# RWKV outputs in tiles of their own, their projection rows during the attention, query-key chunks per pair, later transposes

## The chip, the cores and the metric

The kernel runs on one core of a Trainium2 chip. Its engines work side by side, each through its own queue of instructions in order: PE (TensorE, matrix products and transposes; its weight loads are counted apart as PEld), DVE (VectorE), ACT (ScalarE), POOL (GpSimd) and SP (SyncE, which issues the DMAs). The metric is the device time of one execution in microseconds (us), lower is better.

## The reference, cut to what matters

A decoder trunk of two layers over 512 positions of width 1024, with 256 memory tokens. Each layer normalizes, projects, runs three groups of heads, gates each group, concatenates and projects back. The change lies in the first, the even layer:

```python
def even_layer(h, km, vm, ...):
    qa, ka, va, ga, bs, gb, qm, gm = split_last(h @ w_in, EVEN_SIZES)
    qa = partial_rope(rms_norm(split_heads(qa, A_HEADS), a_qn_g), cos, sin)
    ka = partial_rope(rms_norm(split_heads(ka, A_HEADS), a_kn_g), cos, sin)
    oa = merge_heads(moba_attention(qa, ka, split_heads(va, A_HEADS)))
    ob = rwkv7_time_mix(bs, ...)
    om = memory_attention(rms_norm(split_heads(qm, M_HEADS), m_qn_g), km, vm)
    mixed = jnp.concatenate([oa * silu(ga), ob * silu(gb), om * silu(gm)], axis=-1)
    return mixed @ w_out          # x = x + this
...
    # end of rwkv7_time_mix: y (512 positions, 6 heads of 64)
    mean, var = jnp.mean(y, -1), jnp.mean(jnp.square(y - mean), -1)
    y = (y - mean) * rsqrt(var + eps) * lnx_g + lnx_b
    return y + bonus
```

There are 6 heads of attention, 6 of RWKV and 4 of memory attention, each 64 wide. At 512 positions the block-sparse attention is plain causal attention: a query's own block and all earlier ones are taken.

## The kernel before, in words

**Products.** Every projection is computed in three terms from operands split into a high and a low half (`hi`, `lo` of the weights, `act_hi`, `act_lo` of the activations). `weights` (line 244) brings a block of 256 columns by DMA in pieces of four 128-row tiles (`raw`), makes `hi` by a copy on ACT and `lo` by a subtraction on DVE; the pools are double buffered. `mm3` (line 263) issues the three terms; its matmul is line 269. `projT` makes outputs of 128 rows and 512 columns (24 multiplications), `projN` (line 280) outputs of 128 rows and up to 256 columns. Each output is a `pj` buffer in PSUM, of which there are two.

**The order.** A tile framework gives each engine its queue. Code in a `band` (line 291) has a priority: "g" ahead of "e" (what empties a result), the code's own order, "w" (weight halves), "n" (query and key norms) and "d" (projections). So the projections of a chunk are put between other work wherever the program order leaves PE a place, and nothing overtakes a waiting instruction once the queue is made.

**Even layer.** `first_part` and the rest are written in `even_layer` (line 1021). First come the chunks of the input projection in the order of the string `RWO` (line 40), each under the RWKV work: `l0 k0 r1 v1 r2 v2` are RWKV's inputs, `qm` the memory queries, `q1 q2 q3` and an early `q0` the four column blocks of 256 of queries, keys and values of the causal attention, `g0 g1` gates and values. `nat_chunk` (line 643) keeps a result with positions as rows in `nat0`, and `nat_norm` (line 469) normalizes two or four heads at a time and applies the rotation. A block `q1` holds two query heads and two key heads, `q0` four query heads, `q2` four key heads, `q3` values.

Then RWKV: for each pair of heads q = 0, 1, 2 `rwkv_out` (line 989) computes the outputs from the carried states, `Y` (line 998), subtracts the mean, squares on ACT, forms the reciprocal root in a chain of small DVE operations, scales (line 1010), transposes on PE (line 1013), adds the bonus and multiplies by the gate into `sg[3 + q]`. `Y` and `Yq` are one buffer each for the three q.

Then the attention, in units that `pipeline` (line 630) calls one after another, with steps due some units later (AD = 1 for causal units, ADM = 3 for memory units). `attn_mem_pair` (line 566) has two units for each of two pairs of memory heads: scores (line 503), minimum (line 581), exponential on ACT (line 584), scaling, transposes (line 600), the product with the values (line 609). `attn_causal_pair` (line 531) has four units for each of three pairs: scores, mask and minimum on DVE (line 513), exponential on ACT (line 515), scaling (line 542), transposes (line 549) with their copy to `PT` (527, 529), at the end the product with the values (line 557) and `mix` (line 520), which applies the gate. Before a pair is scored, `load(q)` calls `nat_T` (line 483) for its queries and its keys: four transposes each (line 486), a copy on ACT and a split on DVE (487, 488). `qT` and `kT` have two buffers, by q % 2. Before, `load(0)` was called ahead of all units, `load(1)` and `load(2)` at units and delays that the tuple `PO0` (line 38) gives.

**Output projection.** The gated results are act rows k = 0 to 7: 0 to 2 the three causal pairs, 3 to 5 RWKV, 6 and 7 memory. `split_act` (line 309) makes their halves. `first_part` (line 1144) splits rows 3 to 7 and calls `out_proj` (line 617) for them: four weight blocks of 256 columns, for each four groups of 15 multiplications and an add into `x` (line 623). It is called in the unit that `PO0` gives, 7, with delay 5. After the attention the same is done for rows 0 to 2, groups of 9. Then layer 1 begins with its norm and its transposes (line 461).

Of the kernel before, what the change touches and what calls it, by code (L numbers as in the profile page):

```python
# [11 lines left out]
F32R = mybir.dt.float32r  # L12
# [18 lines left out]
PD_ = 1000000  # L31
AD = 1
# [3 lines left out]
PO0 = (1, 1, 5, 2, 5)  # L36
PO1 = (1, 2, 5, 2, 8, 1, 11, 4, 4)
RWO = 'l0 k0 r1 v1 r2 v2 qm q1 g0 q2 q3 g1'
# [109 lines left out]
def tile_trunk(ctx, tc, x_in, memT_in, w_mem, e_w_in, e_w_out, o_w_in, o_w_out, ln_g, w2_in, a2_in,  # L148
# [95 lines left out]
    def weights(segs, k0=0, nk=KC):  # L244
# [3 lines left out]
        for ka in range(k0, k0 + nk, 4):  # L248
            kb = min(ka + 4, k0 + nk)
# [50 lines left out]
    def chunk(segs, body, k0=0, nk=KC, hot=False):  # L300
        if hot:
            hi, lo = weights(segs, k0, nk)
        else:
            with band("w"):
                hi, lo = weights(segs, k0, nk)
        with band("d"):
            body(hi, lo)
# [188 lines left out]
    def parts(pool, name):  # L496
        return [[tl(pool, [P, S], f"{name}{q}{c}", F32R) for c in "hl"] for q in range(2)]
# [119 lines left out]
    def out_proj(w, x, k0, nk, last=False):  # L617
        for c in range(4):
            def body(hi, lo, c=c):
                for i in range(NT):  # L620
# [6 lines left out]
                    projN(hi, lo, 0, 256, i, act_hi, act_lo, done, range(k0, k0 + nk))  # L627
            chunk([(w, 256 * c, 256)], body, k0, nk)
# [14 lines left out]
    def nat_chunk(w, wc, n, nat, c0, heads=(), hot=False):  # L643
# [16 lines left out]
        chunk([(w, wc, n)], body, hot=hot)  # L660
# [23 lines left out]
    qh = [[(0, 4, "aq")], [(0, 2, "aq"), (2, 2, "ak")], [(0, 4, "ak")], []]  # L684

    def qkv(c, hot=False):
        nat_chunk(ew, EV["qkv"] + 256 * c, 256, nat0, 256 * c, qh[c], hot)
# [12 lines left out]
    with ExitStack() as ph:  # L700
# [30 lines left out]
        qkv(0, True)  # L731
# [44 lines left out]
    def rwkv_tiles(rp):  # L776
        return dict(nr=tl(rp, [P, 4, S], "nr3"), pl=tl(rp, [P, 3, 8], "pl3"), bon=tl(rp, [P, 3, S], "bon3"),
# [211 lines left out]
    def rwkv_out(ip, X, q, sgb):  # L989
# [7 lines left out]
        Y = tl(ip, [P, 8, 64], "Y")  # L997
# [5 lines left out]
        sq = tl(ip, [P, 8, 64], "Yq")  # L1003
# [10 lines left out]
        yy = tl(ip, [P, S], "Yq")  # L1014
# [6 lines left out]
    def even_layer():  # L1021
        sg = [None] * 3 + sg0 + [None] * 2
        with ExitStack() as ph:
            rp = pool(ph, "rp")
            psum_pool(ph, "psr", 1)
            load_cst(rp, "mr", "bo2")
# [3 lines left out]
            X = rwkv_tiles(rp)  # L1030
# [51 lines left out]
            def gb2va(hi, lo):  # L1082
# [7 lines left out]
                q1=lambda: qkv(1), q2=lambda: qkv(2), q3=lambda: qkv(3),  # L1090
                g0=lambda: gate_chunk(ew, [(EV["gb"], sg[3]), (EV["gb"] + P, sg[4])]),
                g1=lambda: chunk([(ew, EV["gb"] + 256, P), (ew, EV["qkv"] + 1024, P)], gb2va),
                qm=lambda: nat_chunk(ew, EV["qm"], 256, qn0, 0, [(0, 4, None)]))
# [8 lines left out]
            with ExitStack() as ips:  # L1102
# [14 lines left out]
        with ExitStack() as ph:  # L1117
# [3 lines left out]
            qT = parts(np_, "qT")  # L1121
            kT = parts(np_, "kT")
            qmT = parts(np_, "qmT")
            for j in range(3):
                sg[j] = tl(np_, [P, S], f"sg{j}")
            gate_chunk(ew, [(EV["ga"], sg[0]), (EV["ga"] + P, sg[1])])
# [30 lines left out]
    with ExitStack() as ph:  # L1157
# [9 lines left out]
        out_proj(e_w_out, x1, 0, 3)  # L1167
# [320 lines left out]
```

## Time and profile before

| | |
|---|---|
| median of 3 runs | 660.4 us (660.39 to 661.84) |
| profiled execution | 660.36 us |
| its span | 658.6 us |
| granted PE clock, every slice | 0.9 or more of full speed |
| start, to 81 us | PE busy 81.00, DVE 60.11 |
| RWKV, 81 to 200 us | PE busy 117.96, DVE 92.75 |
| RWKV end, 228 to 262.14 us | PE busy 33.84 of 34.14, DVE 26.68 |

The span is the time from the first to the last instruction of the profiled execution; what lies around it is 1.8 us here. The windows quoted below give, for a stretch of the span, the busy time of each engine in it and its instructions in brackets. A row of a timeline gives the start, the duration, the engine, the line, the operation, output and inputs, shapes and how many such instructions were joined; a bracket behind it is idle time of the engine ahead of the row and what ended it. Durations of neighbouring matmuls overlap, so prices of them are taken from start to start.

### The profile page before, as it was taken

The numbers are of one execution on the slowest core, as the hardware profiler recorded it, in microseconds if no ns is written. First come the engines' busy times: TensorE is split into PE (matmuls) and PEld (weight loads), VectorE is DVE, ScalarE is ACT, GpSimd is POOL, SyncE is SP. The second block draws the span as 40 slices with busy tenths as digits, with TensorE's granted clock in tenths as the row PEclk, the third lists the DMA queues.
The fourth block names the chain that finished last, engine by engine and source line by source line (L and its number), as shares of the span: only waits on it lengthen the run. The fifth ranks groups of instructions, "written<-read, shape, count | busy, mean of one in ns | idle before, by whom it ended". The sixth has DMA issues, their size and how long they took to land.

```text
span 658.6 us, 15391 instructions
## 1 busy us (share of the span) xinstructions
PE 636.3 (97%) x6192; PEld 549.7 (83%) x6192; DVE 484.9 (74%) x1384; ACT 328.3 (50%) x969; POOL 6.0 (1%) x21
## 2 busy tenths in 40 slices
PE   8899999999999999889999999999999999999997
PEld 5788777898898878656999988779899689978997
DVE  3996775979786488998657985995786775688743
ACT  5567355552231135856425684644573665367220
POOL 1000000000000000000000000000000000000000
PEclk9999999999999999999999999999999999999999
DMA  8462223212220215100434424022232114200323
GB/s 293 135 184 56 66 65 95 72 50 81 66 67 3 66 33 166 42 18 25 136 97 128 124 77 127 3 69 89 71 97 65 34 34 127 65 33 1 97 65 127
DMA packets 62905, 53.52 MB, mean 81 GB/s; under 512 B 3377, under 2 KB 61041, under 8 KB 62834
## 3 DMA queue, kind: packets, MB, share of 16 engines
q1 hardware_dynamic: 62834, 52.55, 26.5%
q8 instruction: 48, 0.79, 0.5%
q14 instruction: 23, 0.19, 0.1%
HBM read 50.44 MB, written 2.10 MB: 80 GB/s over the span
## 4 chain that ended last, share of the span: by engine, by line
PE 70%; DVE 14%; ACT 11%; issue 2%; DMA 2%; SPq 0%; ACTq 0%; DVEq 0%
PE pj L269 52%; DVE lo L260 2%; ACT hi L259 2%; DMA raw<-in_o_w_in_dram 1%; PE s L503 1%; ACT pr L584 1%; PE s L920 1%; PE c L914 1%; PE t L609 1%; PE t L486 1%; ACT pr L515 1%; PE t L1353 1%; DMA memT<-in_memT_dram 1%; PE t L557 1%; PE s L943 1%
## 5 line engine op out<-in xcount | busy, mean ns | idle before, releaser
L259 ACT ACTIVATE hi<-raw 128x512 fp32r<-128x512 f32 (+2 forms) x164 | 89.3, 596 | 87.1 <-PE pj L269 79.1
L260 DVE TENSOR_TENSOR lo<-raw,hi 128x512 fp32r<-128x512 f32 (+2 forms) x164 | 101.2, 648 | 27.8 <-ACT hi L259 13.8
L269 PE MATMUL pj<-hi,act_hi 128*128 128x256 f32 x672 | 101.8, 285 | 0.8 <-ACT sq L654 0.7
L269 PE MATMUL pj<-hi,act_lo 128*128 128x256 f32 x672 | 101.7, 285 | 0.0
L269 PE MATMUL pj<-lo,act_hi 128*128 128x256 f32 x672 | 101.1, 284 | 0.0
L269 PEld LDWEIGHTS pj<-hi,act_hi 128*128 128x128 f32 x672 | 88.7, 188 | 2.8 <-ACT sq L654 0.9
L269 PEld LDWEIGHTS pj<-lo,act_hi 128*128 128x128 f32 x672 | 88.5, 189 | 1.7 <-issue 1.3
L269 PEld LDWEIGHTS pj<-hi,act_lo 128*128 128x128 f32 x672 | 88.6, 189 | 1.1 <-issue 0.6
L269 PE MATMUL pj<-act_hi,lo 128*128 128x512 f32 (+1 forms) x248 | 64.8, 403 | 0.0
L269 PE MATMUL pj<-act_hi,hi 128*128 128x512 f32 (+1 forms) x248 | 64.1, 400 | 0.2 <-ACT act_hi L461 0.2
L269 PE MATMUL pj<-act_lo,hi 128*128 128x512 f32 (+1 forms) x248 | 64.0, 400 | 0.0
L269 PEld LDWEIGHTS pj<-act_lo,hi 128*128 128x128 f32 (+1 forms) x248 | 45.4, 187 | 11.0
L269 PEld LDWEIGHTS pj<-act_hi,hi 128*128 128x128 f32 (+1 forms) x248 | 45.1, 187 | 10.7 <-ACT act_hi L461 0.5
L269 PEld LDWEIGHTS pj<-act_hi,lo 128*128 128x128 f32 (+1 forms) x248 | 44.8, 187 | 10.6 <-issue 0.4
L623 DVE TENSOR_TENSOR x<-pj,x 128x256 f32<-128x256 f32 x64 | 27.0, 422 | 34.1 <-PE pj L269 34.1
L654 ACT ACTIVATE sq<-pj 128x64 f32<-128x64 f32 x144 | 30.2, 229 | 25.4 <-DVE nat L529 15.7
L515 ACT ACTIVATE pr<-pr,mx 128x128 f32<-128x128 f32 (+3 forms) x56 | 31.2, 562 | 12.5 <-DVE mx L513 11.7
L654 ACT ACTIVATION_READ_ACCUMULATOR sq<-pj 128x1 f32 x144 | 29.4, 214 | 0.0
L513 DVE CUSTOM_DVE_ANT_0 pr<-s,mask 128x128 f32<-128x128 f32 (+3 forms) x56 | 25.8, 484 | 3.4 <-PE t L600 1.7
L466 ACT ACTIVATE th<-pj 128x512 f32<-128x512 f32 x16 | 9.6, 598 | 24.1 <-PE pj L269 24.0
L527 ACT ACTIVATE nat<-pj 128x256 f32<-128x256 f32 (+1 forms) x17 | 6.7, 397 | 27.8 <-PE pj L269 27.8
L527 ACT ACTIVATE PT<-t 128x512 f32<-128x512 f32 (+3 forms) x28 | 14.0, 499 | 10.1 <-PE t L600 5.8
(409 smaller groups left out, 1035.5 us busy)
## 6 DMA issues: line engine op xcount, KB each, us to landing
raw<-in_o_w_in_dram SPq DMA_DIRECT2D x20, 512.0 KB, 3.6
raw<-in_e_w_in_dram SPq DMA_DIRECT2D x36, 256.0 KB, 3.1
raw<-in_e_w_in_dram SPq DMA_DIRECT2D x10, 512.0 KB, 4.0
x<-in_x_dram SPq DMA_DIRECT2D x8, 512.0 KB, 7.1
raw<-in_o_w_in_dram SPq DMA_DIRECT2D x16, 256.0 KB, 3.7
raw<-in_o_w_out_dram SPq DMA_DIRECT2D x8, 512.0 KB, 3.4
raw<-in_e_w_out_dram SPq DMA_DIRECT2D x4, 512.0 KB, 3.5
raw<-in_w_mem_dram SPq DMA_DIRECT2D x4, 512.0 KB, 3.6
```

The costliest lines, as they stand in the source:

```text
L259: A.activation(hi[:, z, :n], r, AF.Copy)
L260: V.tensor_tensor(lo[:, z, :n], r, hi[:, z, :n].bitcast(F32), op=OP.subtract)
L269: T.matmul(o, lh(k), rh(k), start=c == 0, stop=c == tot - 1)
L466: A.activation(th, o, AF.Tanh, scale=0.5)
L486: T.transpose(t[:, i * P:(i + 1) * P], nat[:, i, c0:c0 + P], ident)
L503: T.matmul(o, qT[a][h, qs], kT[b][h, ks], start=c == 0, stop=c == 2)
L513: V.tensor_tensor_reduce(pr[:, p, :n], s[:, p, :n], mask[0][:, 384 - i * P:512], 1.0, 1e38, op0=OP.add, op1=OP.min, accum_out=mx[:, p:p + 1])
L515: A.activation(pr[:, p, :n], pr[:, p, :n], AF.Exp, bias=mx[:, p:p + 1], scale=-1.0, accum_out=rs[:, p:p + 1])
L527: A.activation(dst, src, AF.Copy)
L557: T.matmul(o[64 * p:64 * p + 64, j * P:], v[:, j, v0 + q * P + 64 * p:v0 + q * P + 64 * p + 64], PT[p][:, 4 * j:3 * j + 4, :].rearrange("p ...
L623: V.tensor_tensor(x[i][:, cs], o, x[i][:, cs], op=OP.add)
L654: A.activation(sq[:, h0 + h], o[:, 64 * (h0 + h):64 * (h0 + h + 1)], AF.Square, accum_out=ss[:, i * nh + h:i * nh + h + 1])
```

## The change

1. `rwkv_out` writes its results into slices of one tile `Y3` (under the name `AT3`, shared with an earlier buffer), one for each q, and takes its squares and its last product in buffers of different names for different q. The RWKV tiles are allocated ahead of the constants.
2. `first_part` takes act rows 3 to 5 alone, the RWKV outputs, and is called in the second memory unit with delay 0. The rows 6, 7, 0, 1, 2 (`EVK`) are projected in that order after the attention, in groups of 15. `weights`, `chunk` and `out_proj` take a list of rows.
3. The four column blocks `q0` to `q3` are cut otherwise: `pair(q)` holds the two query heads and the two key heads of pair q, from two places of the weights, and `v0` the values. `RWO` changes to `l0 k0 r1 v1 r2 v2 qm g0 g1 v0 q1 q2`, so the gates come ahead of the second and third pair.
4. `load(q)` is called later: `PO0` is gone, and ahead of each causal pair stand empty units, four before pair 0 and two before pairs 1 and 2, with `load(q)` due behind the last of them. So a pair's transposes come after the previous pair's product with the values.

```diff
+EVK = (6, 7, 0, 1, 2)
-PO0 = (1, 1, 5, 2, 5)
-RWO = 'l0 k0 r1 v1 r2 v2 qm q1 g0 q2 q3 g1'
+RWO = 'l0 k0 r1 v1 r2 v2 qm g0 g1 v0 q1 q2'
...
-    def out_proj(w, x, k0, nk, last=False):
+    def out_proj(w, x, ks, last=False):
...
-                first()
+                if first:
+                    first()
...
+    def pair(q, hot=False):
+        segs = [(ew, EV["qkv"] + 384 * j + P * q, P) for j in range(2)]
+        nat_chunk(segs, 256, nat0, 256 * q, [(0, 2, "aq"), (2, 2, "ak")], hot)
...
-    def rwkv_out(ip, X, q, sgb):
+    def rwkv_out(ip, X, q, Y3, sgb):
...
-        Y = tl(ip, [P, 8, 64], "Y")
+        Y = Y3[:, q]
...
-        sq = tl(ip, [P, 8, 64], "Yq")
+        t3 = lambda n: tl(ip, [P, 12, 64], n)[:, :8]
+        sq = t3(("xx", "F", "R1")[q])
...
-        yy = tl(ip, [P, S], "Yq")
+        yy = t3("R2" if q == 1 else "Yq").rearrange("p a t -> p (a t)")
...
-                    nat_T(nat0, q * P, gq["aq"], qT[q % 2])
-                    nat_T(nat0, 384 + q * P, gq["ak"], kT[q % 2])
+                    nat_T(nat0, 2 * q * P, gq["aq"], qT[q % 2])
+                    nat_T(nat0, (2 * q + 1) * P, gq["ak"], kT[q % 2])
...
-            load(0)()
+            def first_part():
+                for k in range(3, 6):
+                    split_act(k, sg[k])
+                out_proj(e_w_out, x1, range(3, 6))
...
-            us[PO0[0]][1].append((PO0[1], load(1)))
+            us[1][1].append((0, first_part))
             for q in range(3):
+                gap = ADM + 1 if q == 0 else AD + 1
+                us[-1][1].append((gap, load(q)))
+                us += [[None, []] for _ in range(gap)]
                 us += attn_causal_pair(ap, qT, kT, nat0, 768, q, sg[q])
...
-            us[PO0[2]][1].append((PO0[3], load(2)))
-            us[7][1].append((PO0[4], first_part))
             pipeline(us)
-            for k in range(3):
+            for k in EVK:
                 split_act(k, sg[k])
...
-        out_proj(e_w_out, x1, 0, 3)
+        out_proj(e_w_out, x1, EVK)
```

The change moves instructions on PE and on DVE. A row below has the line, the operation, output and inputs, the shape and how many such instructions stand in a row; line numbers of the kernel after are 3 to 8 higher. The first place is PE's queue in the last causal pair: transposes of probabilities (`pr`) and projections (`pj`). Before:

```order
L549 MATMUL t_4171<-cident,pr 128x128 x2
L269 MATMUL pj<-lo,act_hi 128x256 x5
L549 MATMUL t_4175<-cident,pr 128x128 x2
L269 MATMUL pj<-hi,act_hi 128x256 x5
L549 MATMUL t_4197<-cident,pr 128x128 x3
L549 MATMUL t_4202<-cident,pr 128x128 x3
L269 MATMUL pj<-hi,act_lo 128x256 x5
L269 MATMUL pj<-lo,act_hi 128x256 x5
L269 MATMUL pj<-hi,act_hi 128x256 x5
L269 MATMUL pj<-hi,act_lo 128x256 x5
L549 MATMUL t_4207<-cident,pr 128x128 x4
L549 MATMUL t_4213<-cident,pr 128x128 x4
```

And now, with the product with the values (64 rows) behind them:

```order
L552 MATMUL t_4120<-cident,pr 128x128
L552 MATMUL t_4141<-cident,pr 128x128 x2
L552 MATMUL t_4145<-cident,pr 128x128 x2
L552 MATMUL t_4167<-cident,pr 128x128 x3
L552 MATMUL t_4172<-cident,pr 128x128 x3
L552 MATMUL t_4177<-cident,pr 128x128 x4
L552 MATMUL t_4183<-cident,pr 128x128 x4
L560 MATMUL t_4189<-PT,nat 64x512 x2
L560 MATMUL t_4189<-PT,nat 64x384 x2
L560 MATMUL t_4189<-PT,nat 64x256 x2
L560 MATMUL t_4189<-PT,nat 64x128 x2
L272 MATMUL pj<-hi,act_hi 128x256 x2
```

Before, projections in groups of five rows stood between the transposes; now no projection stands between the transposes of the last pair, and the first ones of the last part (`hi`, `act_hi`) follow its product with the values.

The second place is PE's queue in the second pair of memory heads (`qmT1`, line 600 before and 603 now its transposes, `pj<-act…` the gates). Before:

```order
L486 MATMUL t_3429<-cident,nat 128x128 x4
L486 MATMUL t_3436<-cident,nat 128x128 x4
L269 MATMUL pj<-act_hi,hi 128x512 x8
L503 MATMUL s<-qn,qmT1h 128x256 x2
L503 MATMUL s<-qn,qmT1l 128x256 x2
L503 MATMUL s<-qn,qmT1h 128x256 x4
L503 MATMUL s<-qn,qmT1l 128x256 x2
L503 MATMUL s<-qn,qmT1h 128x256 x2
L600 MATMUL t_3471<-cident,pr 128x128 x4
L269 MATMUL pj<-act_lo,hi 128x512 x8
```

And now:

```order
L506 MATMUL s<-qn,qmT1h 128x256 x2
L603 MATMUL t_3743<-cident,pr 128x128 x4
L603 MATMUL t_3749<-cident,pr 128x128 x4
L272 MATMUL pj<-act_lo,hi 128x512 x8
L603 MATMUL t_3755<-cident,pr 128x128 x4
L603 MATMUL t_3761<-cident,pr 128x128 x4
L272 MATMUL pj<-act_hi,lo 128x512 x8
L612 MATMUL t_3767<-PT,vm 64x512 x4
L603 MATMUL t_3773<-cident,pr 128x128 x4
L272 MATMUL pj<-act_hi,hi 128x512 x8
L603 MATMUL t_3779<-cident,pr 128x128 x4
L603 MATMUL t_3785<-cident,pr 128x128 x4
```

The transposes of queries and keys (`nat`, line 486 before) have left this place, and groups of eight gate multiplications stand between the transposes of the probabilities and around the product with the values (line 612).

The third place is DVE's queue at the RWKV outputs. Before, the first output's scaling (line 1010) with the beginning of the second (line 998):

```order
L1010 TENSOR_TENSOR Y<-Y,yr 128x512
L260 TENSOR_TENSOR lo<-raw,hi 128x512 x2
L998 TENSOR_TENSOR Y<-c,Yv_556 128x2x4x64
L1016 TENSOR_TENSOR Yq<-Yq,bon_551 128x512
L1000 TENSOR_REDUCE ymu<-Y 128x8
L1017 SCALAR_TENSOR_TENSOR sg_78<-Yq,sg_78 128x512
L1001 TENSOR_SCALAR ymu<-ymu 128x8
```

And now, the beginning of the first two (line 1002) among the norms of a query-key chunk (lines 481 to 484):

```order
L1002 TENSOR_TENSOR AT_3096<-c,Yv_594 128x2x4x64
L483 TENSOR_TENSOR nat<-ru,rz 128x2x8
L1002 TENSOR_TENSOR AT_3096<-s,Yv_594 128x2x4x64
L484 TENSOR_TENSOR nat<-ru,rz 128x2x8
L481 TENSOR_TENSOR ru<-nat,tabqcosx 128x32
L1004 TENSOR_REDUCE ymu<-AT_3096 128x8 x2
L1005 TENSOR_SCALAR ymu<-ymu 128x8
L996 MEMSET s 64x2x64
L1006 TENSOR_TENSOR AT_3096<-AT_3096,ymu 128x512
```

Before, the second output's `Y` came behind the first one's scaling, in the same buffer; now the two begin side by side in slices of `AT`.

More of the change, by code (lines that the diff above doesn't have):

```diff
@@ L242, in rsqrt, with weights @@
         V.scalar_tensor_tensor(r, t, -3.0, r, op0=OP.add, op1=OP.mult)
-    def weights(segs, k0=0, nk=KC):
+    def weights(segs, ks):
         n = sum(w for _, _, w in segs)
@@ L247, in weights @@
         lo = tl(wp, [P, KC, WCOL], "lo", F32R)
-        for ka in range(k0, k0 + nk, 4):
-            kb = min(ka + 4, k0 + nk)
+        starts = [k for n, k in enumerate(ks) if n == 0 or k != ks[n - 1] + 1 or (k - ks[0]) % 4 == 0]
+        for ka in starts:
+            kb = ka + 1
+            while kb in ks and kb not in starts:
+                kb += 1
             raw = tl(wp, [P, 4, WCOL], "raw")
@@ L298, in band, with chunk @@
         tc.cur_priority = keep
-    def chunk(segs, body, k0=0, nk=KC, hot=False):
+    def chunk(segs, body, ks=range(KC), hot=False):
         if hot:
-            hi, lo = weights(segs, k0, nk)
+            hi, lo = weights(segs, ks)
         else:
             with band("w"):
-                hi, lo = weights(segs, k0, nk)
+                hi, lo = weights(segs, ks)
         with band("d"):
@@ L494, in km_parts, with parts @@
         return t[:, 0], t[:, 1]
-    def parts(pool, name):
-        return [[tl(pool, [P, S], f"{name}{q}{c}", F32R) for c in "hl"] for q in range(2)]
+    def parts(pool, name, q):
+        return [tl(pool, [P, S], f"{name}{q}{c}", F32R) for c in "hl"]
     def qk(os, qT, kT, qs, ks):
@@ L626, in done @@
                             nc.sync.dma_start(oi[i][:, cs], x[i][:, cs])
-                    projN(hi, lo, 0, 256, i, act_hi, act_lo, done, range(k0, k0 + nk))
-            chunk([(w, 256 * c, 256)], body, k0, nk)
+                    projN(hi, lo, 0, 256, i, act_hi, act_lo, done, ks)
+            chunk([(w, 256 * c, 256)], body, ks)
     def pipeline(units):
@@ L641, in pipeline, with nat_chunk @@
             n += 1
-    def nat_chunk(w, wc, n, nat, c0, heads=(), hot=False):
+    def nat_chunk(segs, n, nat, c0, heads=(), hot=False):
         def body(hi, lo):
@@ L659, in body @@
                     nat_norm(nat, c0 + 64 * h0, nh, tab, ss)
-        chunk([(w, wc, n)], body, hot=hot)
+        chunk(segs, body, hot=hot)
     def gate_chunk(w, segs):
@@ L730, in tile_trunk @@
         make_tabs(("aq", "ak"))
-        qkv(0, True)
+        pair(0, True)
         lamt = tl(mp, [P, 256], "lam")
@@ L1025, in even_layer @@
             psum_pool(ph, "psr", 1)
+            X = rwkv_tiles(rp)
             load_cst(rp, "mr", "bo2")
@@ L1029, in even_layer @@
             G.memset(rm64.rearrange("p (c t) -> p c t", t=64)[:, :, 0:1], 0.0)
-            X = rwkv_tiles(rp)
             pps = ExitStack()
@@ L1089, in even_layer @@
                 r2=lambda: bs_chunk([("r", 2), ("k", 2)]), v2=lambda: bs_chunk([("v", 2)]),
-                q1=lambda: qkv(1), q2=lambda: qkv(2), q3=lambda: qkv(3),
+                q1=lambda: pair(1), q2=lambda: pair(2),
+                v0=lambda: nat_chunk([(ew, EV["qkv"] + 768, 256)], 256, nat0, 768),
                 g0=lambda: gate_chunk(ew, [(EV["gb"], sg[3]), (EV["gb"] + P, sg[4])]),
                 g1=lambda: chunk([(ew, EV["gb"] + 256, P), (ew, EV["qkv"] + 1024, P)], gb2va),
-                qm=lambda: nat_chunk(ew, EV["qm"], 256, qn0, 0, [(0, 4, None)]))
+                qm=lambda: nat_chunk([(ew, EV["qm"], 256)], 256, qn0, 0, [(0, 4, None)]))
             for n in RWO.split():
@@ L1120, in even_layer @@
             ap = pool(ph, "ap", 4)
-            qT = parts(np_, "qT")
-            kT = parts(np_, "kT")
-            qmT = parts(np_, "qmT")
+            qT, kT = ([None, parts(np_, n, 1)] for n in ("qT", "kT"))
             for j in range(3):
                 sg[j] = tl(np_, [P, S], f"sg{j}")
+            for t, n in ((qT, "qT"), (kT, "kT")):
+                t[0] = parts(np_, n, 0)
+            qmT = [parts(np_, "qmT", q) for q in range(2)]
             gate_chunk(ew, [(EV["ga"], sg[0]), (EV["ga"] + P, sg[1])])
@@ L1424, in odd_layer @@
             ap = pool(ph, "ap1", 3)
-            qT = parts(np_, "qT")
-            kT = parts(np_, "kT")
-            qmT = parts(np_, "qmT")
+            qT, kT, qmT = ([parts(np_, n, q) for q in range(2)] for n in ("qT", "kT", "qmT"))
             def load(h):
@@ L1448, in first_part @@
                     split_act(k, sg[k])
-                out_proj(o_w_out, x1, 4, 4)
+                out_proj(o_w_out, x1, range(4, KC))
             us[11][1].append((PO1[8], first_part))
@@ L1457, in tile_trunk @@
     odd_layer()
-    out_proj(o_w_out, x1, 0, 4, True)
+    out_proj(o_w_out, x1, range(4), True)
 def lay_out(inputs):
```

20 lines of the change are left out of this document (7 added, 13 removed).

## Prediction

> **What bounds the kernel now.** I read the page's engine table first, then the windows by stage, then the timelines of PE, DVE and ACT through the even attention. The page's head:
>
> ```profile
> span 658.6 us, 15391 instructions
> PE 636.3 (97%) x6192; PEld 549.7 (83%) x6192; DVE 484.9 (74%) x1384; ACT 328.3 (50%) x969; POOL 6.0 (1%) x21
> ```
>
> PE is the bound, and the change adds and removes no multiplication. So only stretches in which PE waits or runs at a poor rate can give or cost time. The windows, cut at the first score of the even memory attention, the last projection of pair 2 and the end of the even output projection (columns: PE, PEld, DVE, ACT busy):
>
> ```profile
> core 0: us, PE busy (x) PEld busy (x) DVE busy (x) ACT busy (x) POOL busy (x), PEclk, DMA share, GB/s
> 200.00:262.14 62.14, 60.74 (x715) 50.34 (x713) 40.73 (x98) 18.30 (x34) 0.00 (x0) 1.00 0.23 66
> 262.14:322.23 60.09, 55.35 (x398) 38.88 (x397) 53.88 (x161) 39.77 (x117) 0.00 (x0) 1.00 0.11 34
> 322.23:358.95 36.72, 36.72 (x307) 36.62 (x305) 22.73 (x54) 13.59 (x29) 0.00 (x0) 1.00 0.42 136
> 240.00:260.00 20.00, 20.00 (x95) 16.25 (x94) 14.91 (x41) 7.10 (x14) 0.00 (x0) 1.00 0.41 121
> ```
>
> The attention stretch (60.1 us) is where PE idles: 55.35 busy, 4.7 idle. DVE is busy 53.88 of it, 6.2 idle: the softmax on DVE sets the pace. The 36.7 us behind it are pure projection with PE never idle; that work could have filled the stretch ahead of it. In 240 to 260, where the RWKV outputs stand, PE is busy 20.00 of 20.00.
>
> **The break-even of the attention stretch.** Prices of PE's work, from its timeline:
>
> ```profile
> 240.70 2.04 PE L269 MATMUL pj<-act_hi,lo 128*128 128x512 f32 x8
> 242.58 2.03 PE L269 MATMUL pj<-act_hi,hi 128*128 128x512 f32 x8
> 322.93 0.76 PE L269 MATMUL pj<-lo,act_hi 128*128 128x256 f32 x5
> 323.52 0.76 PE L269 MATMUL pj<-hi,act_hi 128*128 128x256 f32 x5
> 263.76 1.09 PE L486 MATMUL t<-cident,nat 128*128 128x128 f32 x8
> 264.61 2.12 PE L269 MATMUL pj<-act_hi,hi 128*128 128x512 f32 x8
> ```
>
> Start to start, eight of 512 columns take 1.88 us (0.235 each), five of 256 take 0.59 (0.12 each), eight transposes 0.85. Between the first memory score and the last projection of pair 2 the order holds, before against after, 24 against 56 gate multiplications (32 x 0.235 = 7.5), 80 against 152 of the output projection (72 x 0.12 = 8.6) and eight more transposes (0.9): 17.0 us of PE work moves into the stretch. It comes from ahead of it (gates and transposes) and from behind it (304 against 232 projections). So the stretch may last 60.1 + 17.0 = 77.1 us at no change in the total; each us over that is lost, each under it won.
>
> Behind it one thing is new. Every group of the last projection takes act rows 6, 7, 0, 1, 2 in turn, and row 2 is the gated output of pair 2; both pj buffers stand open on it. Before, 160 projections without that row were left. Now PE waits for the mix and the split:
>
> ```profile
> 317.09 0.88 DVE L542 TENSOR_SCALAR pr<-pr,rr 128x512 f32<-128x512 f32 x2
> 317.89 0.68 DVE L260 TENSOR_TENSOR lo<-raw,hi 128x512 fp32r<-128x512 f32 x1
> 319.92 2.38 PE L557 MATMUL t<-PT,nat 128*64 128x512 f32 x16
> 322.35 0.69 DVE L520 SCALAR_TENSOR_TENSOR sg<-t,sg 128x512 f32<-128x512 f32 x1 [1.91 <-PE t L557]
> 323.07 0.63 ACT L310 ACTIVATE act_hi<-sg 128x512 fp32r<-128x512 f32 x1 [3.65 <-DVE sg L520]
> 324.06 0.68 DVE L311 TENSOR_TENSOR act_lo<-sg,act_hi 128x512 fp32r<-128x512 f32 x1
> ```
>
> Projection's end to split's end is 322.3 to 323.7: 1.4 us of bare PE. That leaves 75.7 us for the stretch.
>
> **DVE's work in it.** Added by the order, from the first minimum to the last mix: two more splits of transposed queries and keys, two gates, two weight halves of 512 and three of 256 columns, eleven residual adds (16 against 5), and most of the norm of the third query-key chunk (8 multiplications, 16 rope products, 16 rope sums). Prices, start to start:
>
> ```profile
> 262.69 0.75 DVE L488 SCALAR_TENSOR_TENSOR qT0l<-t,small,qT0h 128x512 fp32r<-128x512 f32 x1
> 263.35 0.74 DVE L488 SCALAR_TENSOR_TENSOR kT0l<-t,small,kT0h 128x512 fp32r<-128x512 f32 x1
> 264.01 0.68 DVE L581 TENSOR_REDUCE mmx<-s 128x2 f32<-128x512 f32 x1
> 318.49 0.68 DVE L529 COPY PT<-t 128x512 f32<-128x512 f32 x1
> 319.10 0.68 DVE L260 TENSOR_TENSOR lo<-raw,hi 128x512 fp32r<-128x512 f32 x1
> 319.69 0.41 DVE L623 TENSOR_TENSOR x<-pj,x 128x256 f32<-128x256 f32 x1
> 320.03 0.41 DVE L260 TENSOR_TENSOR lo<-raw,hi 128x256 fp32r<-128x256 f32 x1
> 158.51 0.49 DVE L473 TENSOR_TENSOR nat<-nat,hr 128x128 f32<-128x128 f32 x2
> 158.92 0.19 DVE L478 TENSOR_TENSOR ru<-nat,tabqcosx 128x32 f32<-128x32 f32 x1
> 159.02 0.19 DVE L479 TENSOR_TENSOR rz<-nat,tabqsinx 128x32 f32<-128x32 f32 x1
> 159.33 0.17 DVE L480 TENSOR_TENSOR nat<-ru,rz 128x16 f32<-128x16 f32 x1
> 159.41 0.17 DVE L481 TENSOR_TENSOR nat<-ru,rz 128x16 f32<-128x16 f32 x1
> ```
>
> That is 0.66 a split of a transpose, 0.60 an operation of 512, 0.34 of 256, 0.20 of 128, 0.10 a rope product, 0.08 a rope sum: 1.3 + 1.2 + 1.2 + 1.0 + 3.7 + 1.6 + 1.6 + 1.3 = 12.9. With 0.7 for small norm operations that now stand ahead of the first minimum, DVE has 53.9 + 13.6 = 67.5 us to do. So 75.7 - 67.5 = 8.2 us of idle DVE is the point at which nothing changes; before it idled 6.2.
>
> **How long DVE will idle.** Before, pair 1's scores run among pair 0's transposes. Now the memory part ends, then pair 0 is loaded, scored, transposed and projected, then pair 1, then pair 2. I walked the three pairs through the order with the prices above and ACT's exponentials (estimates). Pair 2 has nothing beside it: before, between its last scaling (end 317.97) and its mix (322.35) DVE found 2.5 us of copy, weights and adds; now only the copy of 0.6, and the chain is 3.9 long: 3.3, and 1.0 for the wait on the last exponential, 4.3. At the end of pair 0 the projection takes 2.4 and the order puts an add and two weight halves there (0.34 + 0.60 + 0.34): 1.1, with 0.2 at the last exponential 1.3. At the end of pair 1 a split and two weight halves stand there (0.66 + 0.60 + 0.34): 0.8, with 0.6 ahead of it 1.4. From a mix to the next pair's first minimum (transpose, copy on ACT, split, scores) about 3.5 us pass, of which adds and splits fill all but 0.9 for pair 1, and all for pair 2; pair 0 0.2. The memory part: 1.5, where its first projection waits for four exponentials. Together 9.6 us, 1.4 over the point of no change. Ends: 4.3 if only pair 2 waits (-3.9 us), 14 if each of the three pairs waits as long as the last (+5.8).
>
> PE's side of pairs 0 and 1 is nearly as long as DVE's: by the order it carries 99 projections there in groups of three between transposes of 0.1 us. I take 0.5 for it, between 0 and 2.5 (PE and PEld differ by 16.5 us over 60 here, by nothing in 322 to 359).
>
> **The other parts.** RWKV outputs with their own tiles: before, one wait of PE stood in the chain,
>
> ```profile
> 236.03 0.66 PE L1013 MATMUL t<-cident,Y 128*128 128x128 f32 x4 [0.30 <-DVE Y L1010]
> ```
>
> all else was covered by gates. So this gains 0.3 at most. Now the first two outputs' transposes stand together behind fewer gates, while DVE interleaves both chains and pair 1's norm; by the same walk the second waits 0.75. I take +0.4, between -0.3 and +2. Query-key chunks per pair: six norms of two heads for two of four and two of two, 58 more small DVE operations of 0.08 to 0.2; those ahead of 262 lie beside a DVE busy 40.7 of 62.1, nothing. Ten more weight DMAs go through SP's queue; weights are double buffered and 36.7 us of projection showed no wait for them: nothing, at most 0.5. Layer 1's norm starts as before, its transposes now directly behind the projection: 0, between -0.3 and +0.7.
>
> Sum: 1.4 + 0.5 + 0.4 = +2.3, and 0.3 as the middle of the small bounds: +2.6. The profiled execution took 660.36 with a span of 658.6; the median of three is 660.4. So 663.0. About 0.3% (2.0 us) is what a measurement of this kernel can tell from no change.
>
> **A page against the row.** In the stretch PE reads 55.35 of 60.09, PEld 38.88. By PE's reading the floor of the new stretch is 55.4 + 17.0 = 72.4 us, 3.3 under the 75.7. The Trainium skill ("Perfetto Trace Analysis", Identifying the Most-Contended Engine) calls matmul busy time a bad measure and LDWEIGHTS busy the good one; by that the floor would be some 38.9 + 17.0 = 56, and the gain could reach far past 3.3. The row of DVE, with 67.5, decides here: no PE headroom can be used beyond it.
>
> **The rivals.**
> 1. *DVE stays fed (faster).* The adds, weight halves and norm steps now lie in the waits of the memory part and of pairs 0 and 1, and only pair 2's 4.3 remain. Then 67.5 + 4.3 = 71.8 against 75.7: -3.9, held to -3.3 by PE's floor: 657.0 with nothing lost elsewhere. For it: before, DVE idled only 6.2 with far less such filler. Against: each pair now starts from a transpose, a copy and a split in series. It decides when DVE idles under 6.2 us.
> 2. *Idle only moves (same).* DVE idles 7 to 9, the RWKV part loses nothing: 658.4 to 662.4, say 660.7. RWKV's part of the change then does nothing, as its time was covered.
> 3. *Each pair serial (much slower).* As in the walk, with pairs 0 and 1 waiting like pair 2 and PE's switches on top: 666 to 669.
> 4. *The clock drops.* In the windows above the granted clock is 1.00, though PE idles for up to 1.0 us at a time in the stretch:
>
> ```profile
> 267.75 0.39 PE L503 MATMUL s<-qn,qmT1h 64*128 64x256 f32 x2 [1.03 <-DVE lo L260]
> ```
>
> If pair 2's gaps lowered it to half for 3 us of the projection behind, 3/0.24 = 12 multiplications would be done in place of 25: +1.5, 664.5. The Trainium skill ("TensorE: Matmul & The Clock Gate", What's actually happening) has the gate halve the clock after an idle window of about 3.4 us; by that rule gaps of about 2.4 us, as walked, would not do it, and no trace here shows it.
>
> **How the numbers follow.** Forecast with slower by over 0.3% (662.4 to 666): 0.36; rival 3: 0.10; rival 4: 0.04; together 0.50. Same: 0.28. Faster: 0.22, rival 1 and what lies between it and the same. Range 657.0 (rival 1) to 669.0 (top of rival 3). The forecast's own range is 662.4 to 666.
>
> **What would show it.** In the changed profile: first memory score to pair 2's projection longer than 77 us, a bare stretch of DVE and PE of about 4 us around pair 2's last exponential and projection, and a PE wait of about 1.4 us on act_hi behind it; the RWKV region unchanged. Wrong if DVE idles under 6 us there, or if that stretch is under 74.

## The result, and the profile after

The changed kernel takes 668.17 us (median of 4 runs, 667.26 to 670.77), the kernel before beside it 660.89: a ratio of 1.0115, 95% interval 1.0083 to 1.0146. It is slower by 7.3 us. The profiled execution took 670.77 us, 10.4 more than the one of before, and its span is 10.4 longer too. So the profile shows somewhat more than the typical loss. The page's head after:

```profile
span 669.0 us, 15483 instructions
PE 643.1 (96%) x6192; PEld 554.7 (83%) x6192; DVE 486.3 (73%) x1442; ACT 327.2 (49%) x969; POOL 6.1 (1%) x21
```

The same 6192 instructions keep PE busy for 643.1 us in place of 636.3. That is 6.8 of the 10.4 us: multiplications that run slower. PE's idle time grew from 22.3 to 25.9 us (span less busy), which is the other 3.6. The windows after, cut at the same events as before (columns: PE, PEld, DVE, ACT, POOL busy, then the granted clock):

```profile
200.00:254.21 54.21, 53.11 (x733) 46.87 (x729) 43.35 (x158) 20.25 (x77) 0.00 (x0) 1.00 0.22 64
254.21:340.06 85.85, 77.48 (x509) 57.67 (x508) 68.60 (x235) 44.11 (x126) 1.29 (x4) 0.92 0.14 45
254.21:282.10 27.89, 26.43 (x161) 18.55 (x161) 23.67 (x97) 14.19 (x46) 1.29 (x4) 1.00 0.16 55
282.10:301.22 19.12, 17.65 (x136) 14.26 (x134) 17.27 (x53) 10.64 (x30) 0.00 (x0) 1.00 0.11 36
301.22:319.20 17.98, 17.98 (x144) 14.82 (x142) 15.50 (x47) 10.31 (x27) 0.00 (x0) 1.00 0.12 36
319.20:340.06 20.86, 15.42 (x75) 10.05 (x75) 12.16 (x39) 8.97 (x25) 0.00 (x0) 0.67 0.16 46
```

The first memory score comes 7.93 us earlier (254.21 against 262.14); the work that left the part ahead of it was 8.4, so 0.47 was lost there. The attention stretch takes 85.85 us, against 77.1 at no change: 8.76 lost. Behind it (669.0 - 340.06 = 328.94, against 336.37 less the 8.6 moved away) 1.17 was lost. The three make the 10.4.

The last four rows are the memory part and the three pairs. The first three run at a clock of 1.00. In the last pair the granted clock is 0.67, PE is busy 15.42 of 20.86 us and DVE 12.16. PE's timeline there:

```profile
322.64 0.33 PE L506 MATMUL s<-kT0l,qT0h 64*128 64x128 f32 x2 [0.96 <-DVE kT0l L491]
325.02 0.44 PE L506 MATMUL s<-kT0l,qT0h 64*128 64x384 f32 x2 [1.43 <-DVE mx L516]
329.86 1.51 PE L552 MATMUL t<-cident,pr 128*128 128x128 f32 x6 [0.51 <-DVE pr L545]
333.47 1.94 PE L552 MATMUL t<-cident,pr 128*128 128x128 f32 x8 [2.09 <-DVE pr L545]
335.34 4.72 PE L560 MATMUL t<-PT,nat 128*64 128x512 f32 x16
341.50 0.50 PE L272 MATMUL pj<-hi,act_hi 128*128 128x256 f32 x2 [1.44 <-ACT act_hi L313]
```

Between scores, transposes and product stands no projection any more, so PE waits for DVE at each step. The product with the values takes 4.72 us; before it took 2.38. The last row is the wait on act row 2, 1.44 us.

### The profile page after: what moved, and what is told of

Same layout as the page of the kernel before. It is cut to its first block, busy times and chain, and to the rows that moved or that the text cites. A ratio compares the mean times of both kernels' runs of the same rounds, so it can differ in the third digit from the quotient of the medians.

```text
span 669.0 us, 15483 instructions
## 1 busy us (share of the span) xinstructions
PE 643.1 (96%) x6192; PEld 554.7 (83%) x6192; DVE 486.3 (73%) x1442; ACT 327.2 (49%) x969; POOL 6.1 (1%) x21
## 4 chain that ended last, share of the span: by engine, by line
PE 68%; DVE 17%; ACT 7%; DMA 5%; issue 2%; SPq 1%; ACTq 0%
PE pj L272 49%; DVE lo L263 3%; ACT hi L262 2%; PE t L612 1%; DMA x<-in_x_dram 1%; DMA raw<-in_o_w_in_dram 1%; PE s L924 1%; PE c L918 1%; DMA raw<-in_e_w_in_dram 1%; PE t L489 1%; PE s L506 1%; PE t L560 1%; PE t L552 1%; DVE pr L516 1%; DVE act_lo L314 1%
## 5 line engine op out<-in xcount | busy, mean ns | idle before, releaser
L587 ACT ACTIVATE pr<-s,mmx 128x256 f32<-128x256 f32 x32 | 14.9, 484 | 10.6 <-DVE mmx L584 10.6
L372 PE MATMUL pj<-wm,mg 128*128 128x256 f32 x64 | 17.2, 430 | 0.3 <-ACT ksq L383 0.3
```

The lines of the kernel that those rows point to most:

```text
L372: T.matmul(o[i][:, :NM], memT[:, k, i * P:(i + 1) * P], w[:, k, :], start=k == 0, stop=k == KC - 1)
L587: A.activation(pv[:, p, ii, :], sv[:, p, ii, :], AF.Exp, bias=mx[:, c:c + 1], scale=-1.0, accum_out=rs[:, c:c + 1])
```

## The experiments

Theory A at the start: PE runs out of projections in the last pair, idles, its clock halves, and that is most of the loss. Theory B: the late loads put each pair in series, so that DVE and ACT wait, and the clock is a side effect. Each kernel was timed beside the kernel before.

**1. Extra work in the last pair's waits.** The edit, in the last causal pair alone:

```diff
+        def extra(t, n):
+            for _ in range(n):
+                T.matmul(t, kT[q % 2][1][:, 0:P], qT[q % 2][0], start=True, stop=True)
...
+            if warm and i == 1:
+                extra(pj("t"), 5)
...
                t = pj("t")
+                if warm and p == 0:
+                    extra(t, (0, 0, 2, 8)[i])
```

> The kernel after with 15 extra multiplications on PE in the last causal pair (five behind the scores of unit 1, two and eight ahead of the transposes of units 2 and 3), whose results are overwritten unread. They fill PE's waits of 1.43, 0.51 and 2.09 us there. Theory A (the clock): the wait for work in the last pair halves PE's clock from 325.8 to 339.3 us, which makes the product with the values 4.7 us long instead of 2.4 and slows the transposes and scores; with the extra work the clock stays at 1.00 there, the product takes 2.4 and the time falls by 3 to 5 us, to 663 to 665, although work is added. Theory B (the chain of DVE and ACT in the last pair makes the loss, the clock is a side effect beside waits): 667 to 669, no change.

667.2 us (666.6 to 668.58), ratio 1.010 (1.008 to 1.012). That is B's number, but the windows and PE's timeline of this kernel say why it shows little:

```profile
327.69:331.10 3.41, 1.80 (x11) 1.05 (x10) 3.09 (x13) 2.98 (x9) 0.00 (x0) 0.99 0.00 0
331.10:334.50 3.40, 3.39 (x10) 2.41 (x9) 1.47 (x4) 0.49 (x1) 0.00 (x0) 0.51 0.00 0
331.67 3.38 PE L540 MATMUL t<-qT0h,kT0l 128*128 128x512 f32 x8
336.27 2.71 PE L568 MATMUL t<-PT,nat 128*64 128x512 f32 x16 [0.35 <-DVE PT L532]
```

The clock now fell later and for 3.4 us only, and just then the eight extra multiplications stood ahead of the last transposes, on the path. The product is back to 2.71 us, but the extra work took what that gave. So the run does not separate the two theories.

**2. Extra work that gives way.** The same idea at the lowest priority:

```diff
+FILL = ((8,), (5, 5), (5,), (5, 5))
...
             st[i] = pr
+            if q == 2:
+                for n in FILL[i]:
+                    with band("d"):
+                        o = pj()
+                        for k in range(n):
+                            T.matmul(o[:, :256], qT[0][1][:, 0:P], kT[0][1][:, 0:256], start=k == 0, stop=k == n - 1)
```

> The kernel after with 33 extra multiplications of 256 columns on PE in the last causal pair, at the lowest priority, so that they stand where projections would (8 behind the scores of unit 1, 20 between the transposes of units 1 and 2, 5 ahead of those of unit 3); 4.0 us of work whose results nobody reads. In the run with 15 longer ones the clock still fell for 3.4 us, just while 8 of them stood ahead of the last transposes, and they took 3.38 us there against a wait of 2.09. Theory A (half of the loss against a full clock is the clock): no product with the values over 2.8 us in the last pair, clock 0.997 or more in most runs, and 663.5 to 665.5, 2.5 to 4.5 us under after. Theory B (the chain alone): 667 to 669.

665.6 us (664.24 to 667.3), ratio 1.0078 (1.0058 to 1.0098): some 2.5 us less than after, with 4.0 us of useless work added (each kernel had four runs, and the two intervals overlap a little). Its stretch, then the memory part and the three pairs, then the product in the last pair:

```profile
256.19:338.56 82.37, 76.49 (x542) 58.35 (x541) 68.78 (x235) 44.10 (x126) 1.29 (x4) 1.00 0.14 47
256.19:283.90 27.71, 26.27 (x159) 18.39 (x159) 23.50 (x97) 13.99 (x45) 1.29 (x4) 1.00 0.16 57
283.90:303.20 19.30, 17.83 (x138) 14.40 (x135) 17.45 (x53) 10.82 (x30) 0.00 (x0) 1.00 0.11 36
303.20:321.20 18.00, 18.00 (x144) 14.85 (x143) 15.47 (x47) 10.30 (x27) 0.00 (x0) 1.00 0.11 37
321.20:338.56 17.36, 14.39 (x108) 10.71 (x108) 12.36 (x39) 8.99 (x25) 0.00 (x0) 1.00 0.16 54
336.19 2.37 PE L567 MATMUL t<-PT,nat 128*64 128x512 f32 x16
```

The time lies 0.1 us above A's range, and only one of the four runs has the mean clock of 0.997 or more that A asked of most; in the profiled one the drops lie outside the stretch. At a clock of 1.00 the stretch is 82.37 us in place of 85.85: in the profiled executions 3.5 us are the clock's. It still is 5.3 over the 77.1 of no change. So A holds for a part, and waits at full clock make the larger one.

**3. The old rows in the first part.** Late loads stay:

```diff
-EVK = (6, 7, 0, 1, 2)
+EVK = (0, 1, 2)
...
-                for k in range(3, 6):
+                for k in range(3, KC):
...
-                out_proj(e_w_out, x1, range(3, 6))
+                out_proj(e_w_out, x1, range(3, KC))
...
-            us[1][1].append((0, first_part))
...
+                if q == 0:
+                    us[-1][1].append((gap, first_part))
```

> The kernel after with rows 3 to 7 in the first part of the projection, called behind the memory part, and rows 0 to 2 in the last, as before; the late loads and the rest stay. 96 more multiplications (11.5 us) may lie beside the attention. Theory A (PE lacks work beside the last pair, so it idles and its clock halves): the last pair has projections in it, the clock stays 1.00, no bare wait of 1.4 us on the split of row 2; 655 to 660. Theory B (late loads put each pair in series, whatever PE has to do): the stretch grows by what the added work fills and no more, pairs 0 and 1 wait as now; 663 to 667.

658.31 us (656.99 to 660.44), ratio 0.9958 (0.994 to 0.9975): 0.4% faster than before, as A expected. Its stretch and the part behind it, up to layer 1's first transposes:

```profile
253.31:335.03 81.72, 78.03 (x568) 61.87 (x567) 67.90 (x233) 44.04 (x126) 1.30 (x4) 1.00 0.16 52
335.03:359.48 24.45, 24.31 (x199) 23.83 (x199) 19.27 (x54) 14.25 (x30) 0.00 (x0) 1.00 0.51 168
```

The stretch is as long as in the run with useless work (81.72 against 82.37), clock 1.00, but here the projections in it are useful and missing behind it, and PE has no wait on act row 2. The late loads stayed and cost nothing that can be seen.

**4. Early loads.** The empty units go, `load(0)` ahead of the units, `load(1)` and `load(2)` where they were before; rows 3 to 5 stay:

```diff
+            load(0)()
...
-            us[1][1].append((0, first_part))
+            us[1][1] += [(1, load(1)), (0, first_part)]
...
-                gap = ADM + 1 if q == 0 else AD + 1
-                us[-1][1].append((gap, load(q)))
-                us += [[None, []] for _ in range(gap)]
...
+            us[5][1].append((2, load(2)))
```

> The kernel after with the transposes of queries and keys called where they were before (no empty units); the split of the projection by rows and the rest stay. Theory A (PE lacks work at the end, since the first part has only 144 multiplications): DVE idles less in the memory part and in pairs 0 and 1, but the last pair stays nearly bare and the wait on row 2 stays; 663 to 667, clock under 0.995. Theory B (the late loads are the loss): 659 to 661.5.

658.72 us (655.69 to 660.79), ratio 0.9962 (0.9944 to 0.998). B's number, and a little under it. So undoing one half of the change is enough, either the rows (3) or the loads (4): each takes the whole loss away.

**5. Only the last pair early.** `load(2)` in pair 1's first unit, no empty units ahead of pair 2:

```diff
-                us[-1][1].append((gap, load(q)))
-                us += [[None, []] for _ in range(gap)]
+                if q < 2:
+                    us[-1][1].append((gap, load(q)))
+                    us += [[None, []] for _ in range(gap)]
...
+                if q == 1:
+                    us[-4][1].append((0, load(2)))
```

> The kernel after with only the last pair's transposes of queries and keys called early (in pair 1, no empty units ahead of pair 2); loads of pairs 0 and 1 stay late. Theory A (the loss sits in the last pair, which starts when pair 1 is over and finds PE without work): most of the 9 us between after and the kernel with all loads early comes back: 659.5 to 662.5, and the span of pair 2 no longer has a wait of 2 us on PE. Theory B (each late pair loses about the same): a third comes back, 664 to 666.

660.35 us (658.77 to 662.78), ratio 0.9996 (0.9982 to 1.001). As A expected, 7.8 us come back. The stretch, the row on which DVE waits at the end of the memory part, and the longest wait of PE in pair 2 up to its last product:

```profile
253.78:330.46 76.68, 72.37 (x509) 54.97 (x508) 67.61 (x235) 43.93 (x126) 1.28 (x4) 1.00 0.13 44
279.07 0.69 DVE L523 SCALAR_TENSOR_TENSOR sg<-t,sg 128x512 f32<-128x512 f32 x1 [3.21 <-PE t L612]
327.85 2.61 PE L560 MATMUL t<-PT,nat 128*64 128x512 f32 x16 [0.44 <-DVE PT L532]
```

The wait of 2 us on PE in pair 2 is gone, and the clock is 1.00. DVE idles 9.1 us in the stretch (76.68 less 67.61) against 13.6 in experiment 2, although its wait of 3.21 us in the memory part has stayed.

**6. Only the first pair early.** `load(0)` ahead of the memory part, no empty units ahead of pair 0; pairs 1 and 2 stay late:

```diff
+            load(0)()
...
-                gap = ADM + 1 if q == 0 else AD + 1
-                us[-1][1].append((gap, load(q)))
-                us += [[None, []] for _ in range(gap)]
+                if q > 0:
+                    gap = AD + 1
+                    us[-1][1].append((gap, load(q)))
+                    us += [[None, []] for _ in range(gap)]
```

> The kernel after with only the first pair's transposes of queries and keys called early (ahead of the memory part, no empty units ahead of pair 0); pairs 1 and 2 late as in after. Theory A (DVE finds no work at the end of the memory part, where it waits 3.22 us on the last product and 0.62 on a copy, and at the last pair; pairs 0 and 1 cost little): the memory part's 3.8 us come back, the last pair stays bare with its clock halved and the wait on row 2: 663.5 to 665.5. Theory B (the last pair alone is the loss): no more than 1 us comes back, 667 to 668.5.

658.42 us (657.58 to 660.21), ratio 0.9962 (0.9951 to 0.9973). Both theories missed, by 5 us and more. Its windows up to the last pair's first score, and the last pair:

```profile
254.62:313.61 58.99, 56.24 (x401) 42.82 (x400) 54.53 (x191) 35.06 (x101) 1.29 (x4) 1.00 0.11 37
313.61:327.90 14.29, 13.44 (x102) 10.60 (x101) 11.50 (x41) 8.47 (x26) 0.00 (x0) 1.00 0.17 56
```

Nothing was done to the last pair, and yet PE is busy 13.44 of its 14.29 us, at full clock. The memory part and pair 0 now overlap, the stretch is 73.28 us long, and so projections are left when pair 2 comes: 41 stand between its first scores and its product (33 of the first part's 144 and 8 of the last part), where after had none. So it is no loss of one place. It is a balance over the whole stretch, which I formed only now: the chain of DVE and ACT with its waits has a length; PE has a store of projections; when the chain outlasts the store, PE runs bare at the end, and then its clock falls on top. The next table has, from the profiled executions, the time from the first memory score to the last product of pair 2, and to the first projection of layer 1 on its normalized rows. With before's 112.48 plus the 8.4 us moved in, the second of these would be 120.9 at no change. For kernels 4 and 6 it would be 120.0, since there the eight transposes of pair 0 (0.85) stand ahead of the first score again.

| kernel | to the last product | to layer 1's first projection | profiled execution | median |
|---|---|---|---|---|
| after | 85.85 | 130.73 | 670.77 | 668.17 |
| 2, useless work in pair 2 | 82.37 | 126.89 | 667.3 | 665.6 |
| 5, pair 2 early | 76.68 | 122.78 | 662.78 | 660.35 |
| 6, pair 0 early | 73.28 | 119.05 | 658.66 | 658.42 |
| 4, all early | 67.25 | 121.61 | 660.21 | 658.72 |
| 3, more projections | 81.72 | 118.70 | 658.76 | 658.31 |

What the third column has over 120.9 (or 120.0) and what the profiled execution has over before's 660.36 agree within 1 us (for after 9.8 and 10.4), except for 4, where they differ by 1.8. So nearly the whole difference between these kernels lies between the first memory score and layer 1. A shorter chain (4, 5, 6) or a larger store (3) each suffice. Kernel 4 gave part of its gain back behind the stretch: the weights of its last part came late, and the clock fell there.

```profile
330.88 0.79 PE L272 MATMUL pj<-hi,act_hi 128*128 128x256 f32 x2 [1.92 <-ACT hi L262]
321.66:335.00 13.34, 11.34 (x78) 10.92 (x78) 9.44 (x21) 6.79 (x14) 0.00 (x0) 0.87 0.58 179
```

**7. Both remedies.** If there is one loss, repairing it twice gives no more. First the old rows with pair 2 early (edits 3 and 5 together), then the old rows with all loads early (edits 3 and 4), where the first part is called by

```diff
-            us[1][1] += [(1, load(1)), (0, first_part)]
+            us[1][1].append((1, load(1)))
+            us[3][1].append((ADM + 1, first_part))
```

> The kernel after with rows 3 to 7 in the first part of the projection, called behind the memory part, and the last pair's transposes early. The two changes alone gave 658.3 and 660.35. Theory A (one loss, repaired twice: PE without work in the last pair): nothing adds up, 657.5 to 659. Theory B (each change repairs a loss of its own): 654 to 656.

657.98 us (657.28 to 660.02), ratio 0.9959 (0.9946 to 0.9972).

> The kernel after with all transposes of queries and keys early and rows 3 to 7 in the first part of the projection, called behind the memory part (early loads with rows 3 to 5 gave 658.7, late loads with rows 3 to 7 gave 658.3). Theory A (one loss, repaired twice): 657 to 659. Theory B: 654 to 656.

660.42 us (658.72 to 661.97), ratio 0.9988 (0.9977 to 0.9999). Nothing adds up in either, but the second lies above the range of A too. By the slope given at the end, its lower mean clock (0.9957 against 0.9976) makes 0.7 us of the 2.4 between the two; what makes the rest was not found. Kernels 3, 4, 6 and the first of these two beat both after and before, the latter by 0.4%, and can't be told from each other.

**8. A third part of the projection.** Rows 6, 7, 0, 1 beside the last pair, row 2 alone behind it:

```diff
-EVK = (6, 7, 0, 1, 2)
+EVK = (2,)
...
+            def second_part():
+                for k in (6, 7, 0, 1):
+                    split_act(k, sg[k])
+                out_proj(e_w_out, x1, (6, 7, 0, 1))
...
+                if q == 2:
+                    us[-5][1].append((0, second_part))
```

> The kernel after with the rows 6, 7, 0, 1 projected beside the last pair in a part of their own, and row 2 alone behind it: three parts of the projection, so 16 more adds and 16 more weight halves of two rows or fewer on DVE than after. Theory A (PE's lack of work in the last pair is the loss): PE is full there, the clock stays up, only the 1.4 us on row 2 remain, but 16 adds of 0.34 us and the halves come on top on DVE in the attention: 656 to 660. Theory B (late loads put DVE's chain in series, and added work on DVE lengthens it): 662 to 667.

663.68 us (661.91 to 665.19), ratio 1.0043 (1.0029 to 1.0058), in B's range, but mostly not for B's reason: the stretch is 83.28 us long, only 0.9 over experiment 2's. The last pair is full, at a clock of 1.00; the loss moved behind it. The stretch, its last pair, the end of the projection and the longest wait of PE there:

```profile
253.77:337.05 83.28, 79.75 (x574) 62.90 (x573) 70.98 (x241) 44.42 (x126) 1.28 (x4) 1.00 0.15 50
319.00:337.05 18.05, 17.45 (x140) 15.01 (x138) 14.77 (x46) 9.09 (x25) 0.00 (x0) 1.00 0.19 61
350.00:365.18 15.18, 11.75 (x75) 9.49 (x73) 12.34 (x39) 7.71 (x15) 0.00 (x0) 1.00 0.34 113
364.59 0.75 PE L272 MATMUL pj<-hi,mh 128*128 128x256 f32 x4 [1.77 <-ACT hi L262]
```

The row-2 part has groups of three multiplications, each with an add on DVE of 0.42 us, and PE waits for these adds again and again. Layer 1's weight halves (`hi`) stand on ACT behind the squares of its norm, which start only as the adds end.

**9. The RWKV side.** First the change without its attention half. Against after, it has the early loads of edit 4, without its call of `first_part` in `us[1]`, and:

```diff
-EVK = (6, 7, 0, 1, 2)
+EVK = (0, 1, 2)
...
-                for k in range(3, 6):
+                for k in range(3, KC):
...
-                out_proj(e_w_out, x1, range(3, 6))
+                out_proj(e_w_out, x1, range(3, KC))
...
+            us[7][1].append((5, first_part))
```

Then the kernel before with the RWKV outputs' tiles alone (`Y3`, the names of the squares and of `yy`, the RWKV tiles ahead of the constants, word for word as in the change).

> The kernel after with loads and output projection as before, so only the RWKV tiles and the query-key chunks per pair (with their order of chunks) are left of the change. By the comparison of the two traces the part ahead of the first memory score costs 0.45 us (7.93 us gained of 8.4 moved): 660.4 to 661.5, within 0.3% of before. Rival: the chunks per pair put norms on DVE in the attention, where DVE is busy 54 of 60 us: 662 to 664. Other rival: RWKV's own tiles gain and late loads eat it: 658 to 659.5.

659.49 us (658.59 to 663.14), ratio 0.9988 (0.9973 to 1.0003): under the range expected, at the edge of the last rival's.

> The kernel before with the RWKV outputs in tiles of their own and the RWKV tiles ahead of the constants, nothing else. My reading (its waits were covered by gates, 0.3 us at most): 660 to 661.5, no difference. Rival: it carries the gain of 1.5 us that the RWKV side of the change showed: 659 to 659.8.

659.86 us (658.47 to 662.57), ratio 0.9991 (0.9979 to 1.0004). This lies just between the two ranges. Neither kernel differs from before beyond its interval; if there is a gain it is 1 us or so, and which of the two parts carries it stays open. No loss in any case.

## Why the prediction was right in sign and too small in size

The sign, the range and the stretch were right: the loss is in the attention, PE runs bare in its last pair, and the RWKV side costs nothing that can be measured. The size was not: 2.6 us forecast, 7.3 measured, outside the forecast's own range of 662.4 to 666. That 668.17 still lies in the whole range is partly luck. Its top came from rival 3, in which pairs 0 and 1 wait like pair 2, and they did not (1.85 and 2.5 us of idle DVE against 5.0). What came was a wait that no rival had, at the end of the memory part, together with rival 4, the falling clock, which had a chance of 0.04 and cost more than its price.

Term by term, DVE's idle time from the windows of the run with useless work, since its clock is 1.00 (length less busy; the memory part reaches to the first projection on act rows 3 to 5):

| term | forecast | measured |
|---|---|---|
| RWKV part | +0.4 | +0.47 |
| wait on act row 2 | +1.4 | +1.44 |
| DVE's work in the stretch | 67.5 | 68.8 |
| DVE idle, memory part | 1.5 | 4.2 |
| DVE idle, pair 0 | 1.5 | 1.85 |
| DVE idle, pair 1 | 2.3 | 2.5 |
| DVE idle, pair 2 | 4.3 | 5.0 |
| clock in the stretch | 0 | +3.5 |

PE's own 0.5 in pairs 0 and 1 can't be told apart, since these lengths are DVE's work and idle time. Of the 7.8 us by which the profiled loss of 10.4 passed the 2.6, the idle time is 4.0, DVE's work 1.3 and the clock 3.5; the 0.5 and the 0.3 of small bounds did not come on top of them, and behind the stretch 1.17 was lost for the 1.4.

- **The term that was furthest off is the idle time of DVE**, 9.6 forecast and 13.6 measured, and in it the step "The memory part: 1.5, where its first projection waits for four exponentials". No wait of that size for exponentials is there; the two rows of DVE below make 3.84 of the 4.2 us, and of these the walk had 0.2 at pair 0's start. PE's rows show what stands ahead of the product:

```profile
279.50 0.69 DVE L523 SCALAR_TENSOR_TENSOR sg<-t,sg 128x512 f32<-128x512 f32 x1 [3.22 <-PE t L612]
280.81 0.75 DVE L491 SCALAR_TENSOR_TENSOR qT0l<-t,small,qT0h 128x512 fp32r<-128x512 f32 x1 [0.62 <-ACT qT0h L490]
274.21 2.12 PE L272 MATMUL pj<-act_lo,hi 128*128 128x512 f32 x8
276.17 0.60 PE L603 MATMUL t<-cident,pr 128*128 128x128 f32 x4
276.69 2.77 PE L612 MATMUL t<-PT,vm 128*64 128x512 f32 x8
```

  The walk looked at what DVE has to do in each pair, and not at what stands on PE ahead of the memory part's last product: gates of 2.1 us between its transposes, and no pair-0 score yet for DVE to work on, since that pair starts only when the memory part is done. That each pair starts in series was said; that the end of the memory part is such a boundary too got no price. Experiment 6 removes this boundary alone, and the loss is gone. But experiment 5 keeps it, removes another, and the loss is gone as well. So it is the term that was mis-sized, one part of the sum, and not by itself the cause.
- **DVE's work** was 1.3 low; pairs 0 and 1 came out within 0.35 us, pair 2 was 0.7 low, and the wait on row 2 came out as worked out.
- **The clock** was priced at 1.5 us for a drop behind the last pair. It fell inside that pair, for 13.6 us (last section), on the path of its last transposes and its product. The reason given against it, that gaps of 2.4 us would not do it, did not hold: in this pair no wait ahead of the drop was over 1.43 us.
- **The break-even of 77.1 and 75.7 us** held where the same 152 projections stand in the stretch: at full clock after's passed 77.1 by 5.3 (experiment 2), 5 is 1.0 over 75.7 and can't be told from before, 6 is 2.4 under it and faster. In kernels 3 and 4 the traces have 210 and 96 projections there and no wait on row 2, so at 0.12 each the break-even moves to about 84 and 70 us, an estimate; 81.72 and 67.25 are under it.
- Layer 1 differs by little and both ways: from its first projection to the end 284.06 us after, 283.98 before, with a stretch at half clock in it (below) and, in place of before's wait of 1.28 us on `he`, one of 0.25. The first row below is that first projection, the others are the wait in before, then after's windows ahead of the drop and at half clock:

```profile
384.94 1.10 PE L272 MATMUL pj<-act_hi,hi 128*128 128x512 f32 x4
393.76 0.66 PE L1282 MATMUL t<-cident,he 128*128 128x128 f32 x4 [1.28 <-ACT he L1279]
424.70:428.10 3.40, 2.30 (x132) 2.02 (x133) 3.10 (x6) 3.35 (x8) 0.00 (x0) 1.00 0.02 5
428.10:431.50 3.40, 3.40 (x10) 2.62 (x9) 3.40 (x10) 1.93 (x4) 0.00 (x0) 0.50 0.00 0
```

## What to carry to other kernels

Where PE's long queue of independent work hides a chain of another engine, compare the chain's whole length, with its waits at each boundary, with the store of PE's work; lengthening the chain and shrinking the store are each free as long as the balance holds, and together they cost at once. Count the boundaries between serial parts, not the parts. When PE runs bare, price its clock as well: here it was about a third of the loss.

## What the runs showed of the hardware

PE's clock fell without a long pause of PE. The windows of after around the drop, 3.41 us each, and the last one at half clock:

```profile
322.38:325.79 3.41, 1.72 (x20) 1.31 (x20) 2.37 (x12) 1.36 (x7) 0.00 (x0) 0.99 0.43 121
325.79:329.20 3.41, 3.14 (x14) 1.74 (x12) 3.28 (x15) 2.38 (x9) 0.00 (x0) 0.50 0.24 74
336.02:339.43 3.41, 3.41 (x13) 1.93 (x12) 0.00 (x0) 0.02 (x1) 0.00 (x0) 0.51 0.00 0
```

The clock is 1.00 until 325.8 and 0.50 until 339.4, four times 3.4 us. In the 3.41 us ahead PE was busy 1.72, half of them, with no wait over 1.43 us; in experiment 1 the drop came behind 1.80 of 3.41. Yet experiment 2 had a stretch with less, and no drop behind it:

```profile
321.20:324.60 3.40, 1.47 (x13) 1.03 (x13) 3.25 (x6) 2.35 (x4) 0.00 (x0) 1.00 0.33 107
324.60:328.00 3.40, 2.63 (x27) 1.97 (x23) 2.52 (x13) 1.92 (x8) 0.00 (x0) 1.00 0.41 142
```

And after's second drop, at 428.1, came behind a window in which PE was busy 2.30 of 3.40 us, its longest wait 1.09 us. So where such a stretch begins counts, or the busy share is not all that does; the threshold stays open. The Trainium skill ("TensorE: Matmul & The Clock Gate", What's actually happening) has a free-running window of 3413 ns and the halving after an idle one; the length agrees with the trace, that the window must be idle does not. The same page (A second HAM failure mode: psum-queue depth-cycling) tells of a kernel whose many short idles made the clock swing between full and half. These rows agree so far, that the clock halved behind short waits; whether it is the same effect no run here shows.

The mean granted clock varies from execution to execution of one kernel, before's too: in 25 executions it lay between 0.991, with 664.48 us, and 1.000, with 659.77 to 661.77 us. Over 175 executions of 13 kernels, each against the mean of its own kernel, 0.001 of mean clock goes with 0.36 us. After's four stand at 0.987 to 0.992, mean 0.9905, the 74 of before at about 0.9976: by that slope 2.6 of the 7.3 us go with the clock, an estimate that agrees with experiment 2. Kernel 3's and 4's clocks are no higher than before's (0.9962 and 0.9966), so their gain is not the clock's.
